# Token halves at stage turns, a fixed ScalarE order and 14 + 8 weight groups in an encoder layer on one Trainium2 core

## The chip, the core and the metric

The kernel runs on one core of a Trainium2 chip. Its engines run side by side and wait for each other by semaphores: TensorE (PE: matmuls and transposes; PEld: its weight loads), VectorE (DVE), ScalarE (ACT), GpSimd (POOL) and SyncE (SP), whose queue issues the DMAs. Matmuls write to PSUM, which has 8 banks of 128x512 f32. The metric is device time in microseconds, the median of several executions.

## The reference

One layer on 256 tokens of width 2048, all in f32, cut to what matters here:

```python
mod = silu(c) @ w_ada + b_ada            # 2048 x 18432: nine vectors of 2048
sh1, sc1, g1, sh2, sc2, g2, sh3, sc3, g3 = split(mod, 9)
n = rms(h, norm1) * (1 + sc1) + sh1
h = h + 0.5 * g1 * ((silu(n @ w_gate) * (n @ w_up)) @ w_down)      # D_FF = 5632
n = rms(h, norm_mix) * (1 + sc2) + sh2
u, v, c_q, c_kv, k_pe = split(n @ w_in)                            # 1024, 1024, 512, 256, 64
a = gelu(u) * (spatial mix per 128 tokens of rms(gelu(v)))
q, k_nope, v = from c_q and c_kv         # 8 heads of 128 + 64 rotary, values of 128
s = q_nope @ k_nope.T + rotate(q_pe) @ rotate(k_pe).T              # one k_pe for all heads
m = softmax(s * scale) @ v
h = h + g2 * (concat(rms(a), rms(m)) @ w_out)
n = rms(h, norm3) * (1 + sc3) + sh3
h = h + 0.5 * g3 * ((silu(n @ w_gate2) * (n @ w_up2)) @ w_down2)
out = rms(h, final_norm)
```

## The kernel before

**Matmuls.** Each weight tile of 128x2048 f32 (`raw`, five buffers) is loaded by SP and split: ScalarE casts each half to float32r (`whi`, L170), VectorE subtracts (`wlo`, L174). The tokens are held the same way (`nh`, `nl`). A product is hi·nh + hi·nl + lo·nh, so one chunk of four k-tiles is 24 matmuls of 128x512 (12 for each token half t of 128 rows), written by `mm` (L121).

**Feed-forward.** The 22 groups of 256 columns (gate and up side by side in one 128x512 bank for each token half) are split in FIRST = 12 and 10. The first part runs in passes over k: GROUPS (3, 3, 3, 3 and 4 k-tiles) in the first layer, PASSES in the second. At the end of a pass a group's two banks are copied to SBUF (`p<-gu`, the keep-copy, L362) and in the next pass put back by ScalarE (`gu<-p`, the put-back, L366). In the last pass `finish` computes tanh (`th`, L326), `sg` (L327) and `a` (L328); one step later TensorE transposes `a` (`tps`), ScalarE casts it to `s` (L350) and VectorE makes its low part (L351). Of the PSUM banks, four go by turns to even groups and four to odd ones. The second part runs over full k. After each part, four blocks of 512 columns of the down-projection run; `add_out` (L290, L291) multiplies by the gate row `grow`, which four transposes (`tpg`, L239) and a copy make, and adds to `h`. Groups already done free their place, so the first part's kept sums and the activations share buffers.

**Turns.** A turn between stages is the row norm, `TokenNorm`: ScalarE sums the squares of each column block (`sq`, L252), VectorE sums these (L259), POOL takes the power -0.5 (L182, `stats`), VectorE scales (`hn`), TensorE transposes (`tpn`), ScalarE and VectorE make `nh` (L276) and `nl`. Two groups of six matmuls without use (`keep_warm`) stand in the wait. At the end the final norm does the same for the output.

**Mixer.** Scores of a head are a 128-row product of `kT` and a 64-row product of the rotary key `kpeT`, which holds two copies, one in the lower 64 rows for even heads and one in the upper for odd.

**adaLN.** The 144 products of `w_ada` with c run on VectorE (`ada`), spread by the ADA tables over the up-projection, down-projection and mixer.

The order of work on each engine comes from a scheduler in the kernel's language; `tc.issue_after(x)` pins an instruction behind another.

Of the kernel before, what the change touches and what calls it, by code (L numbers as in the profile page):

```python
# [17 lines left out]
P = 128  # L18
# [5 lines left out]
FIRST = 12  # L24
# [3 lines left out]
ADA_UP1 = (2, 2, 3, 2, 2, 3, 2, 2, 3, 2)  # L28
ADA_DOWN1 = ((0, 0, 0, 0, 1, 0), (1, 1, 1, 0, 0))
# [41 lines left out]
def encoder_layer(ctx: ExitStack, tc: tile.TileContext, outx, *, xT, x, pos, cst, vnorm, w_ada, gu1k, gu1, dn1a,  # L71
# [38 lines left out]
    mark = {"stat": 0, "dve": None, "act": None}  # L110
# [52 lines left out]
    def split(src, n=D, cut=D // 2, second=None):  # L163
        raw = rawp.tile([P, D], F32, tag="raw", name="raw")
        sync.dma_start(raw[:, :n], src)
        out = []
        for a, b in ((0, cut), (cut, n)):
# [3 lines left out]
            if a and second is not None:  # L171
                second.tensor_tensor(lo, raw[:, a:b], hi.bitcast(F32), op=ALU.subtract)
            else:
                mark["dve"] = dve.tensor_tensor(lo, raw[:, a:b], hi.bitcast(F32), op=ALU.subtract)  # L174
# [4 lines left out]
    def rstd(ss, n):  # L179
        r = stat(n)  # L180
        dve.tensor_scalar(ss, ss, EPS, None, op0=ALU.add)  # L181
        pool.tensor_tensor(r, ss, half_m[:, :n], op=ALU.pow)  # L182
# [60 lines left out]
    class TokenNorm:  # L243


        def __init__(self):
            self.ss = stat(8)

        def add(self, c):
            for t in range(2):  # L250
                sq = tmp.tile([P, 512], F32, tag="hn", bufs=2, name="sq")
                act.activation(sq, h[:, t, c * 512 : c * 512 + 512], AF.Square, scale=1.0 / math.sqrt(D),  # L252
                               accum_out=self.ss[:, t * 4 + c : t * 4 + c + 1])

        def done(self, warm=False):
            ss = stat(2)
            if warm:
                keep_warm(mark["gu"], 6)
            dve.tensor_reduce(ss, self.ss.rearrange("p (t c) -> p t c", t=2), axis=AX.X, op=ALU.add)  # L259
            if warm:  # L260
                idle = bank("aux", "idle")
                keep_warm(mm(idle[:, :2], ident, ss, True, True), 6)
            self.r = rstd(ss, 2)

        def make(self, n, d0, sh, gs):
            hn = tmp.tile([P, 2, T], F32, tag="hn", bufs=2, name="hn")
            for t in range(2):
                dve.tensor_scalar(hn[:, t], h[:, t, d0 * P : d0 * P + T], self.r[:, t : t + 1], None, op0=ALU.mult)
            ps = bank("aux", "tpn")
            flip4(ps, lambda j, t: hn[:, t, j * P : j * P + P])  # L270
            for j in range(2):
                d = d0 + j
                nr = tmp.tile([P, T], F32, tag="nr", name="nr")
                s, g = mods[:, sh, d : d + 1], mods[:, gs, d : d + 1]
                o = ps[:, j * T : j * T + T]
# [10 lines left out]
    def add_out(banks, c, g, norm=None):  # L286
# [5 lines left out]
        if norm:  # L292
            norm.add(c)
# [811 lines left out]
```

## Time and profile before

| | |
|---|---|
| median of 3 runs | 1841.36 us (1840.18 to 1841.6) |
| the profiled execution | 1839.86 us |
| its span | 1838.1 us |
| mean granted TensorE clock | 0.989 |
| TensorE busy | 1788.3 us, 97% |
| VectorE, ScalarE, POOL busy | 72%, 52%, 2% |

The profile is of one execution; a number of the trace is to be set against 1839.86 us, not against the median. Matmuls overlap, so a busy TensorE may still run below its full pace: the pace is read from starts, not from busy time.

### The profile page before, as it was taken

To read this page: it belongs to the slowest core of one execution; us is meant where nothing else is said; L and a number is where in the kernel's file an instruction comes from. 1 tells how busy PE (TensorE), PEld (TensorE's weight loads), DVE (VectorE), ACT (ScalarE), POOL (GpSimd) and SP (SyncE) were. 2 spreads that over 40 slices of the span, in tenths; PEclk is the share of its full clock that TensorE was granted. 3 is DMA by queue.
4 is the path that set the end of the run, shared out by engine and by line. 5 is a ranking of instruction groups with operands and counts; after the bars stand their busy time and mean duration, and the time that the engine had idled before them with its cause. 6 is when DMAs were issued, how large, how long until landed. Compare 5 with 4: busy or idle time off the path is not lost.

```text
span 1838.1 us, 21587 instructions
## 1 busy us (share of the span) xinstructions
PE 1788.3 (97%) x8078; PEld 1474.0 (80%) x8078; DVE 1329.1 (72%) x1730; ACT 964.8 (52%) x1456; POOL 29.4 (2%) x25
## 2 busy tenths in 40 slices
PE   6999999999999999999999999999999999999996
PEld 4788777888888888888877878888778888888885
DVE  7888878887777778696877886666687855555554
ACT  3788865343444444366675544467654334444442
POOL 1000000000000000001010000000000000000000
PEclk7999999999999999999999999999999999999998
DMA  8989975988778878757856567777568865555551
GB/s 335 332 317 328 339 284 223 356 352 317 301 277 304 311 298 312 286 209 276 313 177 225 192 243 297 261 296 268 181 248 309 320 245 186 196 191 183 183 206 46
DMA packets 70681, 483.52 MB, mean 263 GB/s; under 512 B 7856, under 2 KB 8112, under 8 KB 17584
## 3 DMA queue, kind: packets, MB, share of 16 engines
q1 hardware_dynamic: 70576, 482.14, 71.0%
q8 instruction: 63, 1.03, 0.2%
q14 instruction: 42, 0.34, 0.0%
HBM read 480.01 MB, written 2.10 MB: 262 GB/s over the span
## 4 chain that ended last, share of the span: by engine, by line
PE 54%; issue 41%; DVE 2%; ACT 2%; DMA 0%; POOL 0%; SPq 0%; POOLq 0%; DVEq 0%; ACTq 0%
PE gu L121 25%; PE dn L121 13%; PE wo L121 4%; PE u L121 2%; PE v L121 2%; PE cq L121 1%; PE sc L121 1%; ACT whi L170 1%; DVE ada L132 1%; PE ckv L121 1%; PE qproj L121 1%; DVE wlo L174 0%; PE av L121 0%; DMA xt<-in_xT_dram 0%; PE tpg L239 0%
## 5 line engine op out<-in xcount | busy, mean ns | idle before, releaser
L174 DVE TENSOR_TENSOR wlo<-raw,whi 128x1024 fp32r<-128x1024 f32 (+2 forms) x639 | 747.9, 1181 | 420.4 <-ACT whi L170 415.1
L170 ACT CAST whi<-raw 128x1024 fp32r<-128x1024 f32 (+2 forms) x642 | 648.8, 1019 | 717.2 <-PE gu L121 377.4
L121 PE MATMUL gu<-whi,nh 128*128 128x512 f32 x1408 | 556.2, 395 | 18.3 <-ACT whi L170 12.7
L121 PE MATMUL gu<-whi,nl 128*128 128x512 f32 x1408 | 552.4, 393 | 0.3 <-DVE nl L278 0.3
L121 PE MATMUL gu<-wlo,nh 128*128 128x512 f32 x1408 | 385.1, 391 | 0.0
L121 PE MATMUL dn<-whi,s 128*128 128x512 f32 x1408 | 349.4, 391 | 0.0
L121 PEld LDWEIGHTS gu<-whi,nh 128*128 128x128 f32 x1408 | 266.0, 189 | 79.0 <-ACT whi L170 14.8
L132 DVE CUSTOM_DVE_ANT_0 ada<-ada,cb 128x2048 f32<-128x2048 f32 (+1 forms) x144 | 322.7, 2242 | 0.0
L121 PEld LDWEIGHTS gu<-wlo,nh 128*128 128x128 f32 x1408 | 266.0, 189 | 55.7
L121 PEld LDWEIGHTS gu<-whi,nl 128*128 128x128 f32 x1408 | 266.4, 189 | 54.7 <-DVE nl L278 0.7
L121 PEld LDWEIGHTS dn<-whi,s 128*128 128x128 f32 x1408 | 263.4, 188 | 54.0
L121 PE MATMUL dn<-wlo,s 128*128 128x512 f32 x704 | 188.3, 390 | 0.0
L121 PEld LDWEIGHTS dn<-wlo,s 128*128 128x128 f32 x704 | 132.2, 188 | 27.4
L362 ACT COPY p<-gu 128x512 f32<-128x512 f32 x144 | 77.4, 588 | 30.2 <-PE gu L121 29.9
L366 ACT COPY gu<-p 128x512 f32<-128x512 f32 x144 | 82.3, 598 | 0.4 <-DVE nr L277 0.4
L182 POOL TENSOR_TENSOR stats<-stats,half_m 128x2 f32<-128x2 f32 (+2 forms) x13 | 19.3, 1484 | 1704.9 <-DVE stats L181 1704.9
L290 DVE TENSOR_TENSOR e<-dn,grow 128x512 f32<-128x512 f32 x32 | 20.6, 686 | 20.8 <-PE dn L121 20.8
L121 PE MATMUL wo<-whi,mA 128*128 128x512 f32 x128 | 34.4, 402 | 0.0
L327 DVE SCALAR_TENSOR_TENSOR sg<-th,gu 128x256 f32<-128x256 f32 x88 | 32.9, 416 | 0.3 <-ACT th L326 0.3
L328 DVE TENSOR_TENSOR a<-sg,gu 128x256 f32<-128x256 f32 x88 | 32.9, 416 | 0.0
L121 PE MATMUL wo<-whi,mM 128*128 128x512 f32 x128 | 32.1, 393 | 0.0
L351 DVE TENSOR_TENSOR s<-tps,s 128x512 fp32r<-128x512 f32 x44 | 30.2, 686 | 2.0 <-ACT s L350 2.0
(214 smaller groups left out, 1102.8 us busy)
## 6 DMA issues: line engine op xcount, KB each, us to landing
ada<-in_w_ada_dram SPq DMA_DIRECT2D x144, 1024.0 KB, 5.2
raw<-in_gu_dram SPq DMA_DIRECT2D x140, 1024.0 KB, 4.8
raw<-in_gu_dram SPq DMA_DIRECT2D x44, 768.0 KB, 5.9
raw<-in_dn1a_dram SPq DMA_DIRECT2D x24, 1024.0 KB, 5.4
raw<-in_dn2a_dram SPq DMA_DIRECT2D x24, 1024.0 KB, 5.1
raw<-in_dn1b_dram SPq DMA_DIRECT2D x20, 1024.0 KB, 5.5
raw<-in_win_a_dram SPq DMA_DIRECT2D x20, 1024.0 KB, 6.0
raw<-in_dn2b_dram SPq DMA_DIRECT2D x20, 1024.0 KB, 4.7
```

The source lines that it names most:

```text
L121: return pe.matmul(out, w, x, start=start, stop=stop, skip_group_check=True)
L132: dve.tensor_tensor_reduce(out=w[:, sl], in0=w[:, sl], in1=cb[:, sl], scale=0.5, scalar=acc if i else 0.0, op0=ALU.mult, op1=ALU.add, accu ...
L170: mark["act"] = act.copy(hi, raw[:, a:b])
L174: mark["dve"] = dve.tensor_tensor(lo, raw[:, a:b], hi.bitcast(F32), op=ALU.subtract)
L182: pool.tensor_tensor(r, ss, half_m[:, :n], op=ALU.pow)
L290: dve.tensor_tensor(e, banks[t], g, op=ALU.mult)
L327: dve.scalar_tensor_tensor(s, th, 1.0, g, op0=ALU.add, op1=ALU.mult)
L328: dve.tensor_tensor(a, s, u, op=ALU.mult)
L351: dve.tensor_tensor(lo, ps, hi.bitcast(F32), op=ALU.subtract)
L362: act.copy(part[pg][:, t], banks[t])
L366: act.copy(banks[t], part[pg][:, t])
```

## The change

- FIRST is 14, the parts are 14 and 8 groups; the two ADA tables follow.
- In the last pass of a first part, ScalarE's order is tied: put-backs, the casts behind them, then the cast of `s` and tanh behind the last cast. The cast of `s` and its low part become `store`, which is called later.
- The last chunk of the last column block is written one token half after the other (`end_columns`). `norm.lead(t, ...)` then makes four tiles of `n` for that half alone (`tpl` transposes), and the next stage's first chunk runs by halves too (`first_rows`). POOL gets a small add for each half beside the root. `add_out` writes its product into the PSUM bank and the square goes there too. The second group of useless matmuls goes.
- The gate row is made where it is used, in both parts of each feed-forward, in one buffer.
- `kpeT` has 128 rows for each of even and odd heads, the other half zero (two POOL memsets, one more copy).
- The rotary tables are pinned behind the last weight difference before them.
- At the end, `FinalNorm` scales each half and writes it in four DMAs of 256 KB; `mM` moves to other buffers.

```diff
-FIRST = 12
+FIRST = 14
-ADA_UP1 = (2, 2, 3, 2, 2, 3, 2, 2, 3, 2)
-ADA_DOWN1 = ((0, 0, 0, 0, 1, 0), (1, 1, 1, 0, 0))
+ADA_UP1 = (3, 3, 3, 2, 3, 3, 3, 2)
+ADA_DOWN1 = ((0, 0, 0, 0, 0, 0, 1), (1, 1, 1, 0))
...
+    def behind(instruction):
+        return tc.issue_after(instruction.ins) if instruction is not None else nullcontext()
...
+        def root(self, t):
+            ss, self.r[t] = stat(1), stat(1)
+            pool.tensor_tensor(ss, self.pre[t], self.ss[:, 4 * t + 3 : 4 * t + 4], op=ALU.add)
+            mark["pool"] = pool.tensor_tensor(self.r[t], ss, half_m[:, :1], op=ALU.pow)
...
+        def lead(self, t, sh, gs):
+            self.root(t)
+            hn = tmp.tile([P, 4, P], F32, tag="hn", name="hn")
+            dve.tensor_scalar(hn.rearrange("p a b -> p (a b)"), h[:, t, :512], self.r[t], None, op0=ALU.mult)
+            ps = bank("aux", "tpl")
+            flip4(ps, lambda j, i: hn[:, 2 * j + i])
+            hi, lo = (x[:, :4, token(t)] for x in self.n)
+            for d in range(4):
+                act.activation(hi[:, d], ps[:, d * P : d * P + P], AF.Identity, bias=mods[:, sh, d : d + 1],
+                               scale=mods[:, gs, d : d + 1])
...
+            mark["lead"] = dve.tensor_tensor(lo, nr, hi.bitcast(F32), op=ALU.subtract)
+            mark["hold"] = [None, mark["lead"]]
+        def settle(self, last):
+            keep_warm(mark["gu"], 6)
...
+    def add_out(banks, c, g, norm=None, ts=(0, 1)):
         sl = slice(c * 512, c * 512 + 512)
+        for t in ts:
+            dve.tensor_tensor(banks[t], banks[t], g, op=ALU.mult)
+            last = dve.tensor_tensor(h[:, t, sl], h[:, t, sl], banks[t], op=ALU.add)
+            if norm:
+                norm.add(c, t, banks[t])
+        return last
+    def end_columns(w, banks, xs, c, g, norm, lead):
+        if norm is None or c < 3:
+            wide(w, banks, xs, False, True)
+            add_out(banks, c, g, norm)
+            return
         for t in range(2):
+            wide(w, banks, xs, False, True, (t,))
+            last = add_out(banks, c, g, norm, (t,))
+            lead(t)
+        norm.settle(last)
...
             def take_part(part, pg, banks):
                 for t in range(2):
-                    act.copy(banks[t], part[pg][:, t])
+                    last = act.copy(banks[t], part[pg][:, t])
+                return last
...
-                        take_part(part, pg, new)
-                    w = load()
+                        put = take_part(part, pg, new)
+                    with behind(put if nk == 4 else None):
+                        w = load()
...
+                    last_pass = opens and kt0 and kt0 + nk == KT and i + 1 < len(steps)
+                    store = turn() if not opens or nk == 4 else (lambda: None)
+                    if not last_pass:
+                        store()
                     old = banks
                     if i + 1 < len(steps):
                         w, banks = begin(*steps[i + 1])
                     if kt0 + nk == KT:
-                        finish(pg, old, slots)
+                        with behind(mark["act"] if last_pass else None):
+                            if last_pass:
+                                store()
+                            finish(pg, old, slots)
...
-        kpeT = mix.tile([P, T], F32, name="kpeT")
+        kpeT = mix.tile([P, 2, T], F32, name="kpeT")
...
-                mm(o, qrt[rows, t * P : t * P + P], kpeT[rows], False, True)
+                mm(o, qrt[:, t * P : t * P + P], kpeT[:, j], False, True)
...
+        with tc.issue_after(mark["dve"].ins):
+            rotary_tables(mix.tile([P, 2, 512], F32, tag="g", bufs=2, name="angles"))
```

The next rows are ScalarE's in the last pass of the first up-projection, in the kernel before. A number behind a name is that of the tile; gu_2165 is group 3's bank, gu_2223 and gu_2224 are group 4's, whi_2287 holds group 5's weights.

```order
L170 CAST whi_2287<-raw_2285 128x1024
L170 CAST whi_2291<-raw_2285 128x1024
L366 COPY gu_2223<-p4_1751 128x512
L350 CAST s2_2191<-tps_2216 128x512
L366 COPY gu_2224<-p4_1751 128x512
L326 ACTIVATE th_2237<-gu_2165 128x256
L326 ACTIVATE th_2243<-gu_2166 128x256
L170 CAST whi_2345<-raw_2343 128x1024
```

The same place in the changed kernel, with gu_2728 of group 8 and gu_2844 and whi_2850 of group 10:

```order
L409 CAST s7_2756<-tps_2781 128x512
L384 ACTIVATE th_2802<-gu_2728 128x256
L384 ACTIVATE th_2808<-gu_2729 128x256
L426 COPY gu_2844<-p10_2179 128x512
L426 COPY gu_2845<-p10_2179 128x512
L174 CAST whi_2850<-raw_2848 128x1024
L174 CAST whi_2854<-raw_2848 128x1024
L409 CAST s8_2814<-tps_2839 128x512
```

Before, a group's casts stand one step ahead of its put-backs, and tanh of group 3 behind the put-backs of group 4. Now the put-backs of group 10 stand behind tanh of group 8, and its casts behind these put-backs.

VectorE's rows of the same step in the changed kernel; before, they follow each other in the same way:

```order
L410 TENSOR_TENSOR s7_2756<-tps_2781,s7_2756 128x512
L385 SCALAR_TENSOR_TENSOR sg_2803<-th_2802,gu_2728 128x256
L385 SCALAR_TENSOR_TENSOR sg_2809<-th_2808,gu_2729 128x256
L386 TENSOR_TENSOR a_2804<-sg_2803,gu_2728 128x256
L386 TENSOR_TENSOR a_2810<-sg_2809,gu_2729 128x256
L179 TENSOR_TENSOR wlo_2851<-raw_2848,whi_2850 128x1024
L179 TENSOR_TENSOR wlo_2855<-raw_2848,whi_2854 128x1024
```

What moved against them is ScalarE's put-back of gu_2845, which now stands between this `a` and this wlo.

ScalarE at the first turn between k-passes, before; whi_586 is the weight tile of group 11, p10 the keep-copy of group 10:

```order
L366 COPY gu_618<-p0_315 128x512
L362 COPY p10_596<-gu_551 128x512
L362 COPY p10_596<-gu_552 128x512
L300 ACTIVATE nh_145<-nr_580,mods_77 128x256
L170 CAST whi_586<-raw_584 128x1024
L170 CAST whi_590<-raw_584 128x512
```

And after, where whi_651 is the weight tile of the last group, 13, and p12 the keep-copy of group 12:

```order
L426 COPY gu_682<-p0_314 128x512
L426 COPY gu_683<-p0_314 128x512
L174 CAST whi_651<-raw_649 128x1024
L348 ACTIVATE nh_145<-nr_645,mods_77 128x256
L174 CAST whi_655<-raw_649 128x512
L422 COPY p12_661<-gu_616 128x512
L422 COPY p12_661<-gu_617 128x512
```

The last group's cast stood behind the keep-copy of the group before it and stands ahead of it now.

VectorE at the turn into the mixer, before; dn_5901 and dn_5902 are the banks of the two token halves:

```order
L290 TENSOR_TENSOR e_6082<-dn_5901,grow_155 128x512
L290 TENSOR_TENSOR e_6085<-dn_5902,grow_155 128x512
L291 TENSOR_TENSOR h_2702<-h_2702,e_6082 128x512
L291 TENSOR_TENSOR h_2702<-h_2702,e_6085 128x512
L174 TENSOR_TENSOR wlo_6233<-raw_6226,whi_6232 128x1024
L259 TENSOR_REDUCE stats_78<-stats_78 128x2
L505 TENSOR_SCALAR angles_6392<-cs2_75,stats_78 128x32 x2
L181 TENSOR_SCALAR stats_78<-stats_78 128x2
```

And after:

```order
L325 TENSOR_TENSOR dn_6018<-dn_6018,grow_6033 128x512
L326 TENSOR_TENSOR h_3093<-h_3093,dn_6018 128x512
L325 TENSOR_TENSOR dn_6019<-dn_6019,grow_6033 128x512
L297 TENSOR_SCALAR hn_6165<-h_3093,stats_78 128x512
L326 TENSOR_TENSOR h_3093<-h_3093,dn_6019 128x512
L306 TENSOR_TENSOR nr4_6176<-tpl_6167,mods_77 128x512
L307 TENSOR_TENSOR nr4_6176<-nr4_6176,mods_77 128x512
L297 TENSOR_SCALAR hn_6197<-h_3093,stats_78 128x512
```

The scaling of the first half (hn_6165) now stands ahead of the second half's add, and the rotary tables (`angles`) have left this place.

## Rows read from the trace of the kernel before

**Rows 1.** The page, busy us, share of the span and instructions of each engine.

```profile
PE 1788.3 (97%) x8078; PEld 1474.0 (80%) x8078; DVE 1329.1 (72%) x1730; ACT 964.8 (52%) x1456; POOL 29.4 (2%) x25
```

**Rows 2.** Timeline of TensorE: start, us, operation, count, [idle before, releaser].

```profile
79.87 0.80 PE L121 MATMUL gu<-whi,nh 128*128 128x512 f32 x1 [2.28 <-ACT whi L170]
...
218.13 0.50 PE L121 MATMUL gu<-whi,nh 128*128 128x512 f32 x1 [1.79 <-ACT whi L170]
```

**Rows 3.** The chain that ended last: start, us, engine, work, instructions.

```profile
252.79 4.84 PE gu L121 x20
...
259.25 4.83 PE gu L121 x20
...
338.27 0.44 PE tpg L239 x4
...
471.14 21.79 PE gu L121 x96
```

**Rows 4.** Timeline of ScalarE and VectorE in a last-pass step.

```profile
251.21 1.05 ACT L170 CAST whi<-raw 128x1024 fp32r<-128x1024 f32 x1 [1.44 <-PE gu L121]
...
252.16 0.58 ACT L366 COPY gu<-p 128x512 f32<-128x512 f32 x1
...
252.29 1.22 DVE L174 TENSOR_TENSOR wlo<-raw,whi 128x1024 fp32r<-128x1024 f32 x1 [1.27 <-ACT whi L170]
...
252.68 0.58 ACT L350 CAST s<-tps 128x512 fp32r<-128x512 f32 x1
...
253.44 0.68 DVE L351 TENSOR_TENSOR s<-tps,s 128x512 fp32r<-128x512 f32 x1
...
253.68 0.66 ACT L326 ACTIVATE th<-gu 128x256 f32<-128x256 f32 x2
...
254.76 0.75 DVE L328 TENSOR_TENSOR a<-sg,gu 128x256 f32<-128x256 f32 x2
```

**Rows 5.** Waits of TensorE: who waits, for what, us in all, times, mean.

```profile
PE gu L121 <- ACT gu L366: 5.5, 20, 0.3
```

**Rows 6.** Windows: stretch, length, busy (count) by engine, PEclk, DMA share, GB/s.

```profile
80.00:84.00 4.00, 4.00 (x11) 3.19 (x12) 3.33 (x4) 3.85 (x7) 0.00 (x0) 0.60 0.60 186
320.00:440.00 120.00, 120.00 (x539) 99.42 (x538) 100.67 (x118) 47.84 (x48) 0.00 (x0) 1.00 0.90 346
965.00:1000.00 35.00, 35.00 (x157) 25.51 (x156) 31.00 (x63) 18.46 (x40) 0.00 (x0) 1.00 0.69 246
1022.00:1066.00 44.00, 44.00 (x206) 36.56 (x206) 43.07 (x68) 23.35 (x35) 0.00 (x0) 1.00 0.75 275
```

**Rows 7.** Timeline of TensorE in the attention; two records make up one product.

```profile
949.80 0.70 PE L121 MATMUL sc<-kT,qT 128*128 128x256 f32 x2
950.43 0.70 PE L121 MATMUL sc<-kpeT,qrT 64*128 64x256 f32 x2
...
977.36 1.03 PE L121 MATMUL av<-pp,vat 128*128 128x256 f32 x4
...
978.23 0.59 PE L121 MATMUL sc<-kT,qT 128*128 128x256 f32 x2
```

**Rows 8.** Timeline of all engines at the turn into the mixer.

```profile
774.54 1.29 DVE L290 TENSOR_TENSOR e<-dn,grow 128x512 f32<-128x512 f32 x2 [1.09 <-PE dn L121]
...
776.46 0.63 ACT L252 ACTIVATE sq<-h 128x512 f32<-128x512 f32 x1 [1.55 <-DVE h L291]
...
778.96 0.70 POOL L182 TENSOR_TENSOR stats<-stats,half_m 128x2 f32<-128x2 f32 x1 [733.83 <-DVE stats L181]
...
781.45 0.56 ACT L276 ACTIVATE nh<-tpn,mods 128x256 fp32r<-128x256 f32 x1 [3.66 <-PE tpn L239]
...
794.97 0.93 PE L239 MATMUL tpn<-cs,hn 128*128 128x128 f32 x7
```

**Rows 9.** Timeline of all engines at the end.

```profile
1823.84 1.29 DVE L290 TENSOR_TENSOR e<-dn,grow 128x512 f32<-128x512 f32 x2 [9.25 <-PE dn L121]
...
1828.30 1.95 ACT L1008 ACTIVATE o<-h,stats 128x512 f32<-128x512 f32 x3 [1.21 <-POOL stats L182]
```

More of the change, by code (lines that the diff above doesn't have):

```diff
@@ L1 @@
 import math
[L2 removed]
+from contextlib import ExitStack, nullcontext
 from functools import partial
@@ L265, in make, with open, more, add @@
[L265 to L268, printed above, removed]
+            self.r = [None, None]
+            self.pre = [stat(1), stat(1)]
+            self.n = None
+        def open(self):
+            self.n = new_n()
+        def more(self, c):
+            pass
+        def add(self, c, t, scratch):
+            act.activation(scratch, h[:, t, c * 512 : c * 512 + 512], AF.Square, scale=1.0 / math.sqrt(D),
+                           accum_out=self.ss[:, t * 4 + c : t * 4 + c + 1])
+            if c == 2:
+                dve.tensor_reduce(self.pre[t], self.ss[:, 4 * t : 4 * t + 3], axis=AX.X, op=ALU.add)
+                dve.tensor_scalar(self.pre[t], self.pre[t], EPS, None, op0=ALU.add)
@@ L301, in make_n, with wide @@
         dve.scalar_tensor_tensor(lo, nr, s, hi.bitcast(F32), op0=ALU.add, op1=ALU.subtract)
-    def wide(w, banks, xs, first, last):
+    def wide(w, banks, xs, first, last, ts=(0, 1)):
         half = (len(xs) + 1) // 2
@@ L329, in swiglu, with ffn @@
         return a
-    def ffn(gu, dn, n, gate, ada_pg, ada_dn, lead, groups, prep, norm, before_down=None):
+    def ffn(gu, dn, n, gate, ada_pg, ada_dn, lead, groups, prep, norm, before_down, root):
         with tc.tile_pool(name="actp", bufs=1) as actp, tc.tile_pool(name="ftmp", bufs=2) as ftmp:
@@ L456, in ffn @@
                 kqs = len(slots) // 4
+                if half:
+                    norm.open()
                 for c in range(4):
@@ L459, in ffn @@
                     for kq in range(kqs):
-                        if half == 0 and before_down:
+                        if half == 0:
                             before_down(c, kq)
@@ L463, in ffn @@
                         ada(ada_dn[half][kq])
-                        wide(w, banks, slots[kq * 4 : kq * 4 + 4], kq == 0, kq == kqs - 1)
-                        turn()
-                        if half == 0 and kq == 4:
-                            gate_row(gate, c, grow[:, c])
-                    add_out(banks, c, grow[:, c], norm if half else None)
+                        if kq == (0 if half else 4):
+                            g = gate_row(gate, c)
+                        xs = slots[kq * 4 : kq * 4 + 4]
+                        if kq < kqs - 1:
+                            wide(w, banks, xs, kq == 0, False)
+                        else:
+                            end_columns(w, banks, xs, c, g, norm if half else None, root)
+                        turn()()
+                        if half and c and kq == 1:
+                            norm.more(c - 1)
     with tc.tile_pool(name="ctmp", bufs=2) as ctmp:
@@ L959, in encoder_layer @@
         norm = TokenNorm()
+        norm.open()
         for dp in range(8):
@@ L965, in encoder_layer @@
     norm3 = norm
-    norm3.done(True)
-    n3 = new_n()
+    n3 = norm3.n
     ahead3 = {}
@@ L976, in prep3 @@
     def prep3(kg, pg):
-        if pg == 0 and kg < cut:
-            for d in (kg * 4, kg * 4 + 2):
-                norm3.make(n3, d, SH3, SC3)
+        if pg == 0 and kg == 1:
+            for d in range(4, EARLY, 2):
+                norm3.make(d, SH3, SC3)
         for m, d in ahead3.get((kg, pg), ()):
@@ L985, in prep3 @@
                 if d % 2:
[L986 to L1001 removed]
+                    norm3.make(d - 1, SH3, SC3)
```

187 lines of the change are left out of this document (99 added, 88 removed).

## The prediction

> **What bounds the kernel now.** I read the page's busy table first: TensorE is busy 97% of the span [rows 1], so a change can only pay by removing TensorE's waits, by removing TensorE work, or by shortening the head and the tail. Then the timeline of TensorE and the chain that ended last, to see where full pace is missed. Full pace is 21.79 us for 96 matmuls of 128x512, 0.227 us each; four transposes cost 0.44 us [rows 3]. It is missed at five kinds of places:
>
> First, twice at a turn between weight groups of the first up-projection TensorE waits for a whole cast of weights, 2.28 and 1.79 us [rows 2]. After the first, the granted clock is 0.60 for 4 us, a mixture of the half level (1.2 GHz) and the full one, and 11 matmuls start where 4/0.227 = 17.6 would [rows 6]: 1.5 us more.
>
> Second, in the last pass of both up-projections a step takes 259.25 - 252.79 = 6.46 us [rows 3], where 24 matmuls and four transposes need 24 x 0.227 + 0.44 = 5.89. TensorE waits there for the put-back `gu`, 20 times in all [rows 5], and the second put-back comes late too, which the pipelined busy time hides. The reader sees the cause in [rows 4]: ScalarE waits 1.44 us for TensorE (the next whi overwrites a buffer still being read), then casts for 1.05 us, and the put-back that TensorE needs next stands behind that in ScalarE's queue.
>
> Third, around each stage turn the row norm is a chain through four engines [rows 8]. Fourth, the scores alternate 128-row and 64-row products [rows 7]. Fifth, after TensorE's last bank is read at 1823.84 there are 14.3 us to the span's end [rows 9].
>
> **The change, part by part.** I sum against the profiled execution, 1839.86 us (span 1838.1, 1.76 outside it); the median shown is 1.5 us higher.
>
> *Group turns.* The order of ScalarE before has the keep-copies of group 10 ahead of the cast of group 11; a keep-copy waits for the whole of group 10, so group 11 must start late, however early its weights landed. After, the cast is ahead. Gone: 2.28 + 1.5 + 1.79 = 5.6. Bounds: 0 (the load itself is late) and 6. I take 5.5, because the six vector products of the first group now spread over ten groups instead of eight, which asks less of the queues.
>
> *Last pass.* The new order is put-backs, casts, the cast of the older step's transposes, tanh. Walk one step from a chunk's end (0). The transposes end at 0.44; ScalarE casts s for 0.58, runs two tanh in 0.66 and the first put-back (0.58), to about 2.3. The second put-back takes the bank whose gate half VectorE must have finished with: `a` starts 1.08 us after tanh does, so with the 0.68 us of the low part of s in front the first `a` (half of 0.75) ends near 3.2 [rows 4]. Put-back to 3.8, two casts of 1.05 to 5.9. The next transposes end at 5.89 + 0.44 = 6.3: ScalarE has 0.4 us to spare, and the step is TensorE's 5.89. Gain 20 x 0.57 = 11.4. Bounds: 11.4, or a loss of 4 x 0.57 = 2.3 if the step stays at 6.46 us (14 groups instead of 12 in two layers, 4 steps more).
>
> *14 groups.* 24 more put-backs and 24 more keep-copies lie on ScalarE, at about 0.6 us each [rows 4] some 29 us, beside TensorE, where ScalarE is idle for half of the kernel; the price comes out only where it is the late engine, which is the last pass above. The loads move: SP's queue gets 12 loads of 1 MiB and a piece of x per column of the first down-projection in 7 x 5.45 + 0.44 = 38.6 us, 13.1 MB or 340 GB/s; over the eight groups 22 + 32 loads in 178 us, 318 GB/s; 28 in the second down-projection in 91 us, 324 GB/s. Over 120 us at 346 GB/s TensorE started 539 matmuls, full pace [rows 6]. I take 0; with the cover gone every GB/s short of some 330 costs about 1.3 us of these 423 us.
>
> *Gate rows.* They are kept for one column instead of four, so each layer's second down-projection makes them again: 8 x 0.44 [rows 3] = 3.5 us more on TensorE, nothing beside it. Bounds 3.5 and 3.5.
>
> *Rotary key.* A score product takes 950.43 - 949.80 = 0.63 us, the value product of the same 256 columns with all 128 rows (978.23 - 977.36)/2 = 0.435 [rows 7]. There are 32 score products in 8 calls; the first of a call pays about half, so 5.5 us. VectorE is 31.00 of 35 us busy around half of them [rows 6] and will take some back: I take 4.0, bounds 0 and 5.6. The two memsets and the second copy lie on POOL and ScalarE during the v projection. The Trainium skill, page "TensorE: Matmul & The Clock Gate", section "Step-by-step: what each phase is for", says that a weight load's time goes by columns and that the row count doesn't matter. By that rule 64 rows would be as quick as 128, this part would give 0, and the sum below would be 19.4. The rows disagree with it here.
>
> *Turn into the mixer.* Before, from VectorE's first read (774.54) to the third group's transposes (794.97) 20.4 us pass, for 48 matmuls and 16 transposes, 12.7 us. After, half t0 ends 12 matmuls, 2.7 us, earlier. Its chain: product and add 1.3, square 0.63, POOL's new add (between 0 and the 0.70 of pow, taken 0.4), pow 0.70, and from pow's end to the first nh 781.45 - 779.66 = 1.8 [rows 8]: first nh about 5 us after t0's end. But t1 pays: t0's scaling stands before t1's add on VectorE, t0's four casts before t1's square on ScalarE, POOL does both roots in turn, and six warm-up matmuls stand between t1's transposes and real work. t1's transposes come near 8.9, its last product near 14.6, and then the next four tiles wait for VectorE, where two weight differences stand ahead. I reach the same 48 matmuls near 22.1, 19.4 after the last matmul, with four more transposes done. Gain 1.4, and about 0.6 from the third group's smaller wait: 2.0. The rotary tables leave VectorE's queue here. Bounds: -3 (the clock falls in the wait of 2 to 3 us, as it did in [rows 6]) and 5.
>
> *Turn into the second layer.* The same, but VectorE is 43.07 of 44 us busy ahead of it [rows 6] and gets one more vector product of two 128x1024 halves, about 2.4 us by the wlo of that shape [rows 4]. It reaches the turn about 1 us late: 1.0, bounds -4 and 4.
>
> *End.* Before, 4.5 us to the scaling and 9.8 from there [rows 9]. After, t0's half of the output leaves while t1's root is computed; t1's square waits behind two scalings of t0 on ScalarE (1.3 us). t1 is scaled about 1 us sooner, and half of the bytes are out by then, some 2 us more: 3.0, bounds 0 and 4.5.
>
> Sum: 5.5 + 11.4 - 3.5 + 4.0 + 2.0 + 1.0 + 3.0 = 23.4, so 1816.5 for a profiled execution and, 1.5 us higher, 1818 for the median.
>
> **Rivals.**
> *The last pass is set by a ring of VectorE and ScalarE* (17%). VectorE runs, before as after, the low part of s, two sg, two `a`, two weight differences; in the new order the second put-back stands behind the first `a`, the first cast behind the put-back, the first difference behind the cast. By [rows 4] once round is 0.68 + 0.75 + 0.38 + 0.58 + 1.05 + 2.44 = 5.88 us, as long as TensorE's step. Each 0.1 us more costs 2.8; at 6.46 it is 11.4 + 2.3: 1832. For it: any slow operand in the ring shows at once. Against: a handover costs little (the cast ends at 252.26, the difference starts at 252.29), and an engine starts the next instruction before the last has ended (cast to put-back 252.16 - 251.21 = 0.95 for a cast of 1.05).
> *The turns get longer* (12%). Both bounds together, 3 + 2 and 4 + 1: 1828. For it: t1's chain stands behind t0's on four engines, and the warm-up matmuls come after the wait. Against: t0's matmuls fill part of it.
> *The row count doesn't matter for TensorE* (10%): then the 0.63 us are the price of swapping weights at these operands, which the change keeps, and the time is 1822. Against it is the value product, which swaps at every product too.
> *Slower* (5%): casts no longer run a whole step ahead, so a late put-back now delays the casts behind it. It decides from a step of 5.89 + 23.4/28 = 6.73 us; if put-back and casts went one after the other after VectorE's whole 4.6 us, the step would be about 4.6 + 0.6 + 2.1 = 7.3 and the time 1818 + 28 x 1.4 = 1857. For it: a cast now waits for its put-back by an explicit tie. Against: the walk has 0.4 us to spare, and the second difference has half a step until its turn.
>
> **How the numbers follow.** The forecast has the remaining 56%. Low end: all upper bounds, 6 + 11.4 - 3.5 + 5.6 + 5 + 4 + 4.5 = 33, gives 1808. High end: the two rivals at 1822 and 1828 lie inside, and I stop at 1831, short of the first rival's full price; that and the slower case leave out about 15%. About 0.2% (3.7 us) is what a measurement can tell from no change. All but the last rival lie more than that below: faster 0.93, same 0.02, slower 0.05.
>
> **What would show it.** In the last pass, steps at 5.89 us, and no wait of TensorE for `gu` put-backs; no wait of 2 us near 90 and 250 us; score products 0.435 us apart; 24 copies of `grow`; from t0's end to the third group's transposes about 22 us; about 11 us after the last bank. Steps above 6 us in the last pass, or turns that lose over 8 us, would make the prediction wrong.

## The result and the profile after

The changed kernel takes 1821.55 us (median of 4 runs, 1820.47 to 1821.98); before took 1841.11 us beside it. The ratio is 0.9893 (95% interval 0.9876 to 0.9911), about 20 us faster. The profiled execution has a span of 1819.7 us, 18.4 less than before. Of all executions in this document one, of the kernel with two products moved, took 2569 us at a granted clock of 0.653; it is left out of that kernel's median, and the trace kept for that kernel is of it.

The page's busy table of the changed kernel, against [rows 1]:

```profile
PE 1777.8 (98%) x8082; PEld 1472.5 (81%) x8082; DVE 1324.2 (73%) x1733; ACT 993.8 (55%) x1526; POOL 31.7 (2%) x36
```

Busy time changed by 10.5 us on TensorE and says little. I cut both timelines of TensorE where a stage's first matmul starts (in the mixer and at the ends: where the last one ends) and take off the work that moved: a group of the up-projection is 96 matmuls and four transposes, 21.79 + 0.44 us, a chunk of all four columns of a down-projection 21.79 [rows 3]. Two groups and one chunk for each column went from the second parts to the first.

| stage, us | before | after | work moved | gain |
|---|---|---|---|---|
| to the first `gu` matmul | 20.82 | 20.95 | | -0.13 |
| layer 1, first up-projection | 289.48 | 322.57 | +44.46 | 11.37 |
| layer 1, first down-projection | 133.03 | 156.65 | +21.79 | -1.83 |
| layer 1, second up-projection | 221.94 | 177.81 | -44.46 | -0.33 |
| layer 1, second down-projection | 109.46 | 89.41 | -21.79 | -1.74 |
| last `dn` matmul to the first of v | 49.71 | 48.34 | | 1.37 |
| v to the last `wo` matmul | 251.86 | 247.58 | | 4.28 |
| last `wo` matmul to the 96th `gu` matmul | 31.71 | 32.27 | | -0.56 |
| layer 2, rest of the first up-projection | 251.57 | 290.82 | +44.46 | 5.21 |
| layer 2, first down-projection | 133.04 | 156.63 | +21.79 | -1.80 |
| layer 2, second up-projection | 221.96 | 177.83 | -44.46 | -0.33 |
| layer 2, second down-projection | 109.45 | 89.39 | -21.79 | -1.73 |
| last matmul to the span's end | 14.07 | 9.45 | | 4.62 |

The gains add up to 18.4 us.

TensorE's waits after (for what, us in all, times, longest). Against [rows 5] the put-backs are gone, and of the waits for whi those of [rows 2]; what is left of these lies in the head and at the second turn. New are `dn` and `wo` for wlo, and `tpl`:

```profile
PE gu L124 <- ACT whi L174: 8.8, 4, 3.1
PE tpl L244 <- DVE hn L297: 5.7, 3, 3.0
...
PE dn L124 <- DVE wlo L179: 3.1, 2, 1.6
...
PE wo L124 <- DVE wlo L179: 1.3, 1, 1.3
```

The chain that ended last, in the last pass, against [rows 3]: it was ScalarE, ScalarE, 20 matmuls; it is now TensorE alone, 278.59 - 272.68 = 5.91 us for a step (5.91 and 5.94 by turns through the pass; before, 6.44 and 6.46).

```profile
272.68 5.47 PE gu L124 x24
278.15 0.44 PE tps L244 x4
278.59 5.50 PE gu L124 x24
```

ScalarE and VectorE in that step, against [rows 4]. The chunk ended at 272.1. The reader can follow the new order down ScalarE's rows: s, tanh, put-back, put-back, casts. The second put-back waits 0.69 us for VectorE's `a`, and the next s stands after 1.06 us without work, so the queue keeps up:

```profile
272.72 0.59 ACT L409 CAST s<-tps 128x512 fp32r<-128x512 f32 x1 [2.06 <-PE tps L244]
273.20 0.67 ACT L384 ACTIVATE th<-gu 128x256 f32<-128x256 f32 x2
273.74 0.62 ACT L426 COPY gu<-p 128x512 f32<-128x512 f32 x1
275.05 0.59 ACT L426 COPY gu<-p 128x512 f32<-128x512 f32 x1 [0.69 <-DVE a L386]
275.58 1.99 ACT L174 CAST whi<-raw 128x1024 fp32r<-128x1024 f32 x2
278.63 0.59 ACT L409 CAST s<-tps 128x512 fp32r<-128x512 f32 x1 [1.06 <-PE tps L244]
...
274.61 0.75 DVE L386 TENSOR_TENSOR a<-sg,gu 128x256 f32<-128x256 f32 x2
276.66 2.36 DVE L179 TENSOR_TENSOR wlo<-raw,whi 128x1024 fp32r<-128x1024 f32 x2 [1.31 <-ACT whi L174]
```

What the change lost at the start of a down-projection, on TensorE's timeline: eight matmuls of the first chunk run ahead, then the ninth, the first that needs a low part, waits. Before, VectorE made that low part at 309.49, and the ninth matmul came without a wait:

```profile
309.49 1.23 DVE L174 TENSOR_TENSOR wlo<-raw,whi 128x1024 fp32r<-128x1024 f32 x1
...
310.30 2.09 PE L121 MATMUL dn<-whi,s 128*128 128x512 f32 x8
312.23 1.07 PE L121 MATMUL dn<-wlo,s 128*128 128x512 f32 x4
```

After:

```profile
343.52 2.08 PE L124 MATMUL dn<-whi,s 128*128 128x512 f32 x8
347.17 1.20 PE L124 MATMUL dn<-wlo,s 128*128 128x512 f32 x4 [1.57 <-DVE wlo L179]
```

ScalarE's casts, the first two of this chunk, and VectorE at the same time. The chunk's weights were cast by 341.8 us, but its first wlo stands in VectorE's queue behind the last group's sg and `a`, which can't start before that group's chunk has ended:

```profile
338.88 2.96 ACT L174 CAST whi<-raw 128x1024 fp32r<-128x1024 f32 x3
...
342.62 0.08 DVE L135 DVE_READ_ACCUMULATOR2_ANT mods<- 128x1 f32 x1
343.81 0.42 DVE L385 SCALAR_TENSOR_TENSOR sg<-th,gu 128x256 f32<-128x256 f32 x1 [1.11 <-ACT th L384]
344.56 0.69 DVE L410 TENSOR_TENSOR s<-tps,s 128x512 fp32r<-128x512 f32 x1 [0.33 <-ACT s L409]
...
345.89 1.22 DVE L179 TENSOR_TENSOR wlo<-raw,whi 128x1024 fp32r<-128x1024 f32 x1
```

At the turn into the mixer, against [rows 8], t0's transposes come 1.45 us after TensorE ran dry, eight of its twelve products (those without `nl`) run from 770.03 to 772.1, and t1's transposes are late again (start, us, operation, idle before):

```profile
768.85 0.63 PE L244 MATMUL tpl<-cs,hn 128*128 128x128 f32 x4 [1.45 <-DVE hn L297]
...
773.45 0.66 PE L244 MATMUL tpl<-cs,hn 128*128 128x128 f32 x4 [1.31 <-DVE hn L297]
```

At the turn into the second layer it is VectorE that comes late: a weight difference stands between the product and the add of t0, and the granted clock of the 15 us behind the last matmul is 0.77, with single matmuls 0.43 us apart for a while, where it is 1.00 behind the first turn. VectorE's timeline there:

```profile
1061.57 0.69 DVE L325 TENSOR_TENSOR wo<-wo,grow 128x512 f32<-128x512 f32 x1
1062.17 1.22 DVE L179 TENSOR_TENSOR wlo<-raw,whi 128x1024 fp32r<-128x1024 f32 x1
1063.30 0.68 DVE L326 TENSOR_TENSOR h<-h,wo 128x512 f32<-128x512 f32 x1
```

TensorE's, where t0's transposes wait 2.98 us:

```profile
1066.30 0.97 PE L244 MATMUL tpl<-cs,hn 128*128 128x128 f32 x4 [2.98 <-DVE hn L297]
...
1068.40 0.63 PE L124 MATMUL gu<-wlo,nh 128*128 128x512 f32 x1
1068.83 0.63 PE L124 MATMUL gu<-whi,nh 128*128 128x512 f32 x1
```

And three windows (columns as in [rows 6]), behind the first turn, ahead of the second and behind it:

```profile
767.00:782.00 15.00, 11.03 (x57) 7.80 (x55) 10.57 (x20) 7.88 (x18) 1.82 (x4) 1.00 0.24 86
1035.00:1064.00 29.00, 27.06 (x122) 21.72 (x120) 28.07 (x43) 13.40 (x20) 0.00 (x0) 1.00 0.93 343
1063.00:1078.00 15.00, 11.47 (x49) 9.21 (x48) 9.12 (x17) 5.90 (x14) 1.47 (x4) 0.77 0.36 139
```

The scores, against [rows 7]: all products have 128 rows and start 0.43 us apart.

```profile
956.13 0.59 PE L124 MATMUL sc<-kpeT,qrT 128*128 128x256 f32 x2
956.57 0.59 PE L124 MATMUL sc<-kT,qT 128*128 128x256 f32 x2
957.00 0.59 PE L124 MATMUL sc<-kpeT,qrT 128*128 128x256 f32 x2
```

The end, against [rows 9]: t0's read starts 2.7 us ahead of t1's, t0 is scaled from 1810.67 and t1 from 1813.55, where 4.46 us passed before from the last bank to the scaling and now 3.25.

```profile
1807.58 0.70 DVE L325 TENSOR_TENSOR dn<-dn,grow 128x512 f32<-128x512 f32 x1 [6.75 <-PE dn L124]
...
1810.30 0.70 DVE L325 TENSOR_TENSOR dn<-dn,grow 128x512 f32<-128x512 f32 x1 [1.30 <-PE dn L124]
1810.67 1.33 ACT L1100 ACTIVATE o<-h,stats 128x512 f32<-128x512 f32 x2 [0.92 <-POOL stats L274]
...
1813.55 1.33 ACT L1100 ACTIVATE o<-h,stats 128x512 f32<-128x512 f32 x2 [0.93 <-POOL stats L274]
```

### The profile page after: what moved, and what is told of

It reads as the page before. It is cut to its first block, busy times and chain, and to the rows that moved or that the text cites. A ratio compares the mean times of both kernels' runs of the same rounds, so it can differ in the third digit from the quotient of the medians.

```text
span 1819.7 us, 21634 instructions
## 1 busy us (share of the span) xinstructions
PE 1777.8 (98%) x8082; PEld 1472.5 (81%) x8082; DVE 1324.2 (73%) x1733; ACT 993.8 (55%) x1526; POOL 31.7 (2%) x36
## 4 chain that ended last, share of the span: by engine, by line
PE 92%; DVE 4%; ACT 2%; issue 1%; DMA 1%; POOL 0%; SPq 0%; ACTq 0%; POOLq 0%; DVEq 0%
PE gu L124 52%; PE dn L124 26%; PE wo L124 3%; PE u L124 2%; PE v L124 2%; DVE ada L135 1%; PE tps L244 1%; DVE wlo L179 1%; PE cq L124 1%; PE ckv L124 1%; PE sc L124 1%; ACT whi L174 1%; PE qproj L124 1%; PE tpg L244 1%; DMA raw<-in_wout_dram 0%
## 5 line engine op out<-in xcount | busy, mean ns | idle before, releaser
L174 ACT CAST whi<-raw 128x1024 fp32r<-128x1024 f32 (+1 forms) x646 | 647.8, 1013 | 648.7 <-PE gu L124 295.6
L426 ACT COPY gu<-p 128x512 f32<-128x512 f32 x168 | 96.5, 603 | 16.6 <-DVE a L386 16.0
L422 ACT COPY p<-gu 128x512 f32<-128x512 f32 x168 | 89.7, 586 | 14.7 <-PE gu L124 14.5
L409 ACT CAST s<-tps 128x512 fp32r<-128x512 f32 x44 | 25.8, 587 | 32.8 <-PE tps L244 32.8
L325 DVE TENSOR_TENSOR dn<-dn,grow 128x512 f32<-128x512 f32 x32 | 20.9, 694 | 17.2 <-PE dn L124 17.2
L384 ACT ACTIVATE th<-gu 128x256 f32<-128x256 f32 x88 | 29.0, 384 | 7.7 <-PE gu L124 7.7
```

The source lines that it names most:

```text
L174: mark["act"] = act.copy(hi, raw[:, a:b])
L384: act.activation(th, g, AF.Tanh, scale=0.5)
L409: act.copy(hi, ps)
L422: act.copy(part[pg][:, t], banks[t])
L426: last = act.copy(banks[t], part[pg][:, t])
```

## The experiments

My theory after the result: ScalarE's tie, the group count and the rotary key give what they were priced at, the tie brings a new wait at the first down-projection chunk, and the turns give little because t1's chain stands behind t0's. The rivals are in each expectation. All edits are to the changed kernel, each run has its ratio to the kernel before.

**The tie taken out (e1_untied).**

```diff
-                    with behind(put if nk == 4 else None):
+                    with behind(None):
...
-                    last_pass = opens and kt0 and kt0 + nk == KT and i + 1 < len(steps)
+                    last_pass = False
```

> The changed kernel without the tie on ScalarE in the last pass (put-backs, casts, s and tanh in the order that they had before); everything else as changed. Theory: the tie is what brought the step from 6.46 to 5.9 us, so 13 of 14 steps in each layer get 0.55 us longer again, 26 x 0.55 = 14 us; the wait of the first down-projection chunk for its wlo, 2 x 1.6 us in the changed kernel, may go with the tie. So 1832 to 1836 us. Rival: the 14 groups or the other buffers removed the lateness and the tie does nothing: 1821 to 1822 us.

Measured: 1829.96 us, ratio 0.9943 (0.993 to 0.9957). The first up-projection takes 329.50 us instead of 322.57, and in the second layer, from its first matmul, 325.05 instead of 318.59: 13.4 us for 26 steps, 0.52 each. The chain is again cast, put-back, 20 matmuls:

```profile
272.35 1.06 ACT whi L174
273.40 0.49 ACT gu L426
273.89 0.04 issue
273.94 4.83 PE gu L124 x20
```

Both first down-projections take 154.79 instead of 156.65 us: the wait for wlo goes with the tie. So the tie gives 13.4 and takes 3.7, 9.7 in all. The time is 8.4 us longer than the changed kernel's, below the 10 to 14 that I expected: a late step cost 0.52 and not 0.55, the wait for wlo cost 1.86 a layer and not 1.6, and the out projection was 1 us shorter than in the first profile.

**Key in 64 rows (e2_key64).**

```diff
-                mm(o, qrt[:, t * P : t * P + P], kpeT[:, j], False, True)
+                mm(o, qrt[rows, t * P : t * P + P], kpeT[rows], False, True)
...
```

(cut: the tile of the key and its copies are those of before, too)

> The changed kernel with the rotary key in 64 rows, as before. Theory: a score product after a 64-row one is 0.2 us dearer, the mixer from the v projection on gets about 4.3 us longer (what the two traces differ by there) and the time is 1825 to 1827 us. Rival: the row count of the product doesn't matter, the mixer's gain came from elsewhere: 1821 to 1822 us.

Measured: 1826.72 us, 0.9924 (0.9912 to 0.9937). The products stand 0.63 us apart again, those of 128 rows among them:

```profile
957.57 0.70 PE L124 MATMUL sc<-kpeT,qrT 64*128 64x256 f32 x2
958.20 0.70 PE L124 MATMUL sc<-kT,qT 128*128 128x256 f32 x2
958.83 0.70 PE L124 MATMUL sc<-kpeT,qrT 64*128 64x256 f32 x2
```

The weight loads show what changes. A load of 64 rows is no slower than one of 128: the median is 184 ns here and 190 ns in the changed kernel, 32 loads each. But in the changed kernel the loads of a product start 0.21 us ahead of it (955.92 and 956.13 us), beside the product before, while here both start at 957.57, after 0.33 us in which the profile shows nothing that they waited for:

```profile
955.92 0.41 PEld L124 LDWEIGHTS sc<-kpeT,qrT 128*128 128x128 f32 x2
...
957.57 0.29 PEld L124 LDWEIGHTS sc<-kpeT,qrT 64*128 64x128 f32 x2 [0.33 <-issue]
958.20 0.30 PEld L124 LDWEIGHTS sc<-kT,qT 128*128 128x128 f32 x2 [0.33 <-issue]
```

The first row is of the changed kernel. No run has only 64-row products, so whether it is the 64 rows or the change of the row count that holds a load back is open.

From u to the first `wo` matmul, with two of the eight calls, 73.57 us instead of 72.07, as before. The rest, 3.3 us, lies in the out projection, where kernels that change nothing there differ by up to 4 us (116.23 to 120.26): the pitch is certain, the total only to a few us.

**12 and 10 groups (e3_first12).** The edit is FIRST and the two tables of before.

> The changed kernel with 12 and 10 groups and the two tables of adaLN products that go with them. Theory: the cast of the last group of the first k-passes stands behind a keep-copy again, two waits of about 2 us and a stretch at a lower clock come back, 5 to 6 us in all: 1826 to 1828 us. Rival: the order at the turns does not depend on the group count, or more groups in passes cost as much on ScalarE and the queue as the turns gain: 1819 to 1822 us.

Measured: 1826.51 us, 0.9924 (0.9912 to 0.9937). The first up-projection takes 282.66 us where 322.57 - 44.46 = 278.11 is the same without the two groups: the turns cost 4.55. In layer 2, whose passes show no such waits, the same segment differs by 0.3. TensorE's waits from 60 to 300 us (for what, us in all, times, longest) are again those two, where the changed kernel has none:

```profile
PE gu L124 <- ACT whi L174: 4.1, 2, 2.3
```

But the stretch at a lower clock didn't come back: from 80 to 84 us, behind the same wait of 2.28 us, the granted clock is 1.00, where it was 0.60 in [rows 6]. So the waits at the group turns come from the count, by the order that it leads to, and more groups in passes cost nothing that shows.

**Whole chunks at the turns (e4_turns_whole).**

```diff
+        end = type(norm) is not TokenNorm
+        if not end:
+            wide(w, banks, xs, False, True)
         for t in range(2):
-            wide(w, banks, xs, False, True, (t,))
+            if end:
+                wide(w, banks, xs, False, True, (t,))
```

(and the first chunk behind a turn in the old order)

> The changed kernel with both token halves together again in the last chunk before each turn and in the first chunk behind it; the end of the kernel keeps its halves, and the norm of four tiles for each half stays. Theory: at the turn into the mixer t0's chain starts 2.7 us later and TensorE waits that much longer, less what t1 had to wait, so 1 to 3 us there; at the second turn VectorE is the late engine and the halves give nothing: 1822 to 1825 us. Rival: t1's chain behind t0's costs more than the overlap gives, so that whole chunks are quicker: 1818 to 1821 us.

Measured: 1828.42 us, 0.9939 (0.9926 to 0.9951). Neither: 51.87 us at the turn into the mixer (48.34 with halves) and 34.43 to the 96th matmul at the second (32.27). TensorE waits 4 us at each, and the clock is 0.77 behind both, where with halves it was 1.00 at the first and 0.77 at the second:

```profile
768.00:783.00 15.00, 9.23 (x39) 7.76 (x40) 10.11 (x18) 4.67 (x14) 1.58 (x4) 0.77 0.19 70
1071.00:1086.00 15.00, 8.98 (x38) 7.38 (x38) 10.11 (x18) 4.61 (x13) 1.58 (x4) 0.77 0.27 112
```

The halves are worth 3.5 and 2.2 us there, against the same chain of four tiles for each half. Against the kernel before, which made two tiles for both halves, the gain is 1.4 and -0.6, so most of it is spent again by what else changed at the turns. That it is this chain of four tiles is likely, but no run takes it apart. The other 4 us of this run lie in the v projection (1.6) and the out projection (2.2) and stay unexplained.

**Down-projection's first weights split early (e5_down_first).** The split of the first chunk, and the gate product ahead of it, are issued before the last group's `finish`:

```diff
+                    else:
+                        after()
...
+            def first_down(half):
+                if half == 0:
+                    before_down(0, 0)
+                early.append(split(dn[half][0, 0]))
...
```

> The changed kernel with the split of the first down-projection chunk issued ahead of the last group's sg and a, in all four down-projections. Theory: in the changed kernel the first wlo of the down-projection stands behind the last sg on VectorE, since the last group's casts come late in the tied order; TensorE waits 1.6 us for it and the segment is 1.85 us longer in each layer. With the wlo ahead, 3.7 us go: 1817 to 1819 us. Rival: the weights themselves come late (raw buffers free late in the tied order), and the wait stays: 1821 to 1822 us.

Measured: 1818.58 us, 0.9884 (0.9871 to 0.9897). The wait at the first chunk is gone; half of the loss stays (155.73 us where 133.03 + 21.79 = 154.82 would be no loss), now at the second chunk, whose wlo stands behind the second gate product:

```profile
352.76 1.20 PE L124 MATMUL dn<-wlo,s 128*128 128x512 f32 x4 [0.64 <-DVE wlo L179]
```

That the time fell into the expected range is in part luck: of the 3.7 us only 1.8 came there, and another 1.0 lies at the second turn, which the edit doesn't touch (31.24 us instead of 32.27, at a clock of 0.89 instead of 0.77).

**Two products moved (e6_products_moved).**

```diff
-    "ckv": (2, 1, 0, 1), "v0": (0, 1, 0, 1), "v1": (1, 0, 0, 0),
+    "ckv": (2, 1, 0, 1), "v0": (0, 1, 0, 1), "v1": (1, 1, 1, 0),
...
-    "outA": (0, 1, 1, 2, 0, 0, 0, 0), "outM": (1, 1, 1, 1, 1, 1, 1, 0),
+    "outA": (0, 1, 1, 2, 0, 0, 0, 0), "outM": (1, 1, 1, 1, 1, 0, 0, 0),
```

> The changed kernel with two adaLN products moved from the end of the out projection to the second v projection. Theory: at the turn into the second layer VectorE is the late engine (busy 28.07 of 29 us ahead of it, a weight difference between the product and the add of the first half); with 4.5 us less there, the turn is 1 to 3 us shorter and the clock falls less: 1819 to 1821 us. Rival: the wait at this turn is the norm's own chain, and the time stays at 1821 to 1822 us.

Measured: 1817.78 us, 0.9879 (0.9864 to 0.9893), a little more than expected. Its trace can't be set against the others, so where the gain lies is seen only in the combined kernels below.

**Whole last chunk (e7_end_whole).** As for the turns, but for the last norm alone.

> The changed kernel with both token halves together in the last chunk of the whole kernel; the turns keep theirs, and so do the eight DMAs of 256 KB and the norm for each half. Theory: of the 4.6 us that the end got shorter, the halves carry most, since t0's half of the output leaves 2.7 us later: from the last matmul to the end 11 to 12 us instead of 9.45, 1823 to 1825 us. Rival: t1's chain ends last in both, and the order of halves ahead of it gives nothing: 1821 to 1822 us.

Measured: 1825.06 us, 0.9919 (0.9906 to 0.9932). From the last matmul to the end 12.00 us instead of 9.45. So of the end's 4.62 us the halves give 2.55; the other 2.07 come from the rest of that part (root of one half at a time, gain of three columns applied ahead, smaller DMAs), which I didn't take apart. In this profile another 2.4 us lie in the out projection, which the edit doesn't touch, and the six executions spread from 1821.04 to 1830.39 us, so only the end itself is certain.

**t1's square on VectorE at the turns (e9_square_on_vector).**

```diff
...
+            if c == 3 and t == 1 and type(self) is TokenNorm:
+                dve.tensor_tensor_reduce(out=scratch, in0=x, in1=x, scale=1.0 / D, scalar=0.0, op0=ALU.mult,
+                                         op1=ALU.add, accum_out=acc)
...
```

> The changed kernel with t1's square of the last column at the two turns on VectorE, right behind the add, instead of on ScalarE behind t0's four casts. Theory: t1's chain is what TensorE waits for at the turn, and its square waits 1.6 us for the casts of t0; without that the second transposes come 1 to 1.6 us earlier at each turn: 1819 to 1820 us. Rival: VectorE is as late as ScalarE there, or the wait goes over to the scaling behind it: 1821 to 1823 us.

Measured: 1818.23 us, 0.9881 (0.9868 to 0.9894). The turns take 47.09 us (48.34) and 29.95 (32.27), 3.6 in all. At the first the clock is 1.00 as in the changed kernel, and t1's transposes start 4.80 us after the last matmul instead of 6.06: there t1's chain is what the turn waits for. At the second the clock is 1.00, too, where it was 0.77, so part of the 2.3 us can be the clock's.

**The changed kernel once more (c0_changed_again).**

> The changed kernel once more, beside the next three on the same chip: 1820 to 1823 us, and the segments of its trace within 0.3 us of those of the first profile, but for the out projection, which differed by up to 3 us between kernels that don't change it.

Measured: 1820.53 us, 0.9899 (0.9885 to 0.9912). The turn into the mixer is 48.34 again and the second 32.20, the clocks 1.00 and 0.77 again; of the segments two differ by more than 0.3 us, the first up-projection by 0.32 and the out projection by 0.55.

**Three edits together (b1_three_edits).** The edits of e5, e6 and e9.

> The changed kernel with three edits together: the first down-projection chunk split ahead of the last group's sg and a, two adaLN products moved from the out projection to the second v projection, and t1's square at the turns on VectorE. If each gain is in a place of its own, they add: 3.0 + 3.7 + 3.3 = 10 us, 1811 to 1813 us. Rival: the second and the third edit both shorten the same wait at the turn into the second layer, and only 7 to 8 us come: 1814 us.

Measured: 1814.52 us, 0.9867 (0.9854 to 0.9881), 6 us less than the changed kernel beside it and a little less than the rival's 7 to 8. The second turn takes 28.38 us (29.95 with the square alone): t0's transposes wait 1.46 us there instead of 3.02, and the out projection's wait for wlo is gone. With the 0.8 us that the out projection is shorter, the two products give 2.4 us here, where alone they gave 3.8. That is on the rival's side; but the first up-projection also took 1.2 us longer in this profile, which stays unexplained.

**Gate products behind the split (b2_gate_product_behind).**

```diff
+                        w = early.pop() if early else split(dn[half][c, kq])
                         if half == 0:
                             before_down(c, kq)
-                        w = split(dn[half][c, kq])
...
```

(against the changed kernel; cut: the gate product ahead of the early split goes, too)

> The kernel with the three edits, but each gate product of the first half's down-projection is issued behind the chunk's own split and not ahead of it. Theory: what is left of the loss at the start of the down-projection (0.9 us in each layer) is the second chunk's first weight difference, which waits behind the second gate product; with the product behind the split it goes, 1.8 us less than the kernel with three edits. Rival: the weights then land later, since the loads change places in the queue, or the gate row comes late, and nothing is gained.

Measured: 1811.64 us, 0.9848 (0.9835 to 0.9862). Both first down-projections take 154.79 us, so no loss is left there: 1.9 us less than in the run before, for the two, of the 2.9 by which the time is shorter. The turns take 48.37 and 29.60 us, 1.25 and 1.2 longer than in the run before with the same code there: the clock was 0.89 in both, 1.00 in the other.

**No useless matmuls (b3_no_warm).**

```diff
-            keep_warm(mark["gu"], 6)
+            pass
```

> The kernel of the run before without the six matmuls that are of no use at each turn. Theory: they stand ahead of t0's products with nl, which are ready about 1.2 us before TensorE gets to them; without them each turn is about 1 us shorter, 2 us in all. Rival: TensorE idles there instead, the granted clock falls from 1.00 as it did with whole chunks at the turns (0.73 and 0.66), and each turn gets 1 to 3 us longer.

Measured: 1812.54 us, 0.9859 (0.9845 to 0.9873). No difference that can be measured. The clock stayed at 1.00 in both turns, against the rival; the second turn takes 28.14 us, the first 47.87, against 28.38 and 47.12 with them and the clock at 1.00. Whether they pay is open.

## Why the prediction was right

It said 1818 us with 1808 to 1831, and the time is 1821.55. By its own terms:

- *Group turns, 5.5 us:* 6.2, the 11.37 of layer 1 less the 5.21 of layer 2, which has no such turns. Right: 4.6 of it, the two waits, came back in the run with 12 groups; the other 1.6 is about the price that I put on the stretch at a clock of 0.60, which did not come back there.
- *Last pass, 11.4 us:* 5.2 in each layer, 10.4; the steps went from 6.45 to 5.92 us where I had 6.46 and 5.89. Right. The walk through the step was on the careful side: the second put-back began 2.97 us after the chunk's end and 1.06 us were to spare, where I had 3.2 and 0.4. The ring of VectorE and ScalarE did not set the step.
- *14 groups, 0:* the loads kept up. The second up-projections are 0.33 us each over their share, but the run with 12 groups has the same (222.29 and 221.94 us before), so this isn't the count's price.
- *Gate rows, -3.5:* -1.74 and -1.73. Right.
- *Rotary key, 4.0:* 4.28 in the mixer, of which the out projection's own scatter of some us is part; the pitch went from 0.63 to 0.43 us and back with the one edit, and a 64-row product slowed the 128-row products next to it as well. The rival that the row count doesn't matter is out by this pitch, although its time, 1822, was met: that is chance. The page "TensorE: Matmul & The Clock Gate" of the Trainium skill, section "Step-by-step: what each phase is for", has a weight load's time go by columns and not by rows. The trace agrees with it, 184 ns for a load of 64 rows and 190 for one of 128. The rows that I had read, the pitch of products, disagree with what I drew from the rule and not with the rule: what costs there is when a load starts, not how long it takes.
- *Turns, 2.0 and 1.0:* 1.4 and -0.6, inside their bounds. The second turn is a term that I mis-sized: I charged VectorE's lateness with 1 us, but a whole weight difference stood in the middle of t0's chain, and the clock of the turn was 0.77 behind a wait of 3 us. That t1's chain sets the first turn is shown by the run with its square on VectorE (1.25 us at the same clock); at the second turn the clock moved as well. The sign that I gave for the first turn, about 22 us from t0's end to the third group's transposes, was missed: it took 23.3. The 48th product is no earlier than before (20.8 us after the last `dn` matmul, 20.4 before), so the 1.4 us are gained behind it and not where the walk had them.
- *End, 3.0 us:* 4.6, just over its bound of 4.5. The mechanism was right, by the run with a whole last chunk for 2.55 of it; my price for the rest was too low.

The missing term is the first chunk of the down-projection, -3.6 us in both layers together. The prediction asked what stands behind a late put-back within the pass, but not what follows the pass's last step. With the tie the first weight difference of the next stage stands on VectorE behind the last group's sg and `a`, which wait for that group's tanh; without it, and before, it stands ahead of them. Why the scheduler places it so, no run shows. I had named what is queued behind a put-back, and stopped at the pass's edge. With this term the sum would have been 19.8, and the median 1821.6.

That this meets the 1821.55 is in part luck. The terms of the sum came to 22.8 instead of 23.4 because their errors cancel (the end and the group turns 2.3 more, the last pass and the turns 3.2 less), another 0.8 are lost in stages that the sum left out, and the gain between the two profiles is 18.4. It is 20 between the medians, since the changed kernel's profiled execution lies at its median and that of before lay 1.5 us under the one that I used.

The kernel with the three edits and the gate product behind the split (1811.64 us) is faster than both, by about 9 us against the changed one beside it.

## What to carry to other kernels

When an order is tied within a pass, follow each queue past the pass's end: the first instruction of the next stage, which the scheduler used to put early, may now stand behind work that waits. Price a stage by cutting both timelines at the same matmuls and taking off the work that moved; busy shares and totals hide gains and losses of the same size. When work is halved to start a chain earlier, look for what of the second half stands behind the first on each engine; here one square on another engine gave 3.6 us at the two turns (at the second the clock moved as well), where the whole change had gained 0.8.

## What the runs showed that I had not expected

The granted clock at the turns hangs on little. At the second turn TensorE waits 2.9 to 3.0 us for t0's transposes in eight profiles, and the clock of the 15 us from the last matmul is 0.77 in four (the changed kernel twice, without the tie, with 12 groups), 0.89 in three (64-row key, first weights split early, whole last chunk) and 1.00 in one (square on VectorE). Of these, two rows:

```profile
1062.30:1077.30 15.00, 11.27 (x55) 8.87 (x55) 9.97 (x18) 6.90 (x16) 1.48 (x4) 0.89 0.29 113
1062.00:1077.00 15.00, 11.66 (x61) 9.15 (x62) 11.93 (x22) 7.29 (x16) 1.48 (x4) 1.00 0.40 146
```

The first is of the kernel with the first weights split early, the second of the one with the square on VectorE. Where the turn's code is the same, it takes 32.0 to 32.3 us at 0.77 and 31.2 at 0.89, so an edit elsewhere can seem to gain 1 us that is the clock's. With the same code at both turns the kernel with three edits had 1.00 and the next, which differs only in the order of queues in the down-projections, 0.89; the price was 1.25 and 1.2 us. At the first turn, too, it was 1.00 in some kernels and 0.89 in others with the same code there. What decides the clock stays open; with the six useless matmuls taken out it was 1.00.

The out projection, where VectorE is busy for 28.07 of the last 29 us, took between 116.2 and 120.3 us in kernels with the same work there.
